# Tile-wise waits on reused places, one transposition on VectorE, and later steps in a decoder trunk

## The chip, the cores and the metric

One core of a Trainium2 chip runs the whole program. The metric is the device time of one execution in microseconds. TensorE is called PE here (PEld its weight loads), VectorE DVE, ScalarE ACT, GpSimd POOL, SyncE SP; transfers are issued from SP.

## What is computed

Two layers on 2048 tokens of width 1024. Layer one: every token is normed and projected to small latents (c_q, c_kv, an index key, index weights, a gate z). An index scores all earlier keys, the best 256 of each query are taken, and eight heads attend to those. Layer two: a gated delta rule with eight heads, chunk by chunk, which needs the inverse of a triangular matrix per chunk. After each layer comes an output projection and a gated embedding of the token. Cut from the reference:

```python
def dsa_mixer(h, ...):
    c_q, c_kv, k_idx, w_idx, z = jnp.split(h @ w_in, ...)
    c_q = rms_norm(c_q, g_cq)
    q_lat = einsum("bshd,hdl->bshl", einsum("bsc,chd->bshd", c_q, w_uq), w_uk)
    q_lat = rms_norm(q_lat, g_q) * (D_C ** -0.5)
    c_kv = rms_norm(c_kv, g_kv)
    score = einsum("bqhs,bqh->bqs", relu(q_idx @ k_idx), w_idx)
    sel = top_k(causal(score), 256)
    o_lat = attention(q_lat, c_kv[sel], rel_bias)
    return (einsum("bshl,hlv->bshv", o_lat, w_uv) * silu(z)) @ w_out
def chunked_gated_delta_rule(q, k, v, g, beta):
    # S_t = a_t S_{t-1} (I - b_t k_t k_t^T) + b_t v_t k_t^T,  o_t = S_t q_t
```

## The kernel before

The program is one stream of steps per engine, written by generators. Each generator yields a number, its place in the stage, and `weave` merges several generators in the order of these numbers; so a constant in a `yield` moves all that stands behind it on every engine. Products of float32 are made as three products of split halves (lines L90, L91, L92 in stage one, L1521 to L1523 in the delta net).

Places in memory come from pools by tag: `T(tag, bufs, ...)` takes the next of `bufs` places of that tag, and waits for whoever used it last. A `scope` opens a pool and gives it back at its end; what is allocated next from the same memory waits for the released pool as a whole.

The stages, by the time of the profile:
- latents (0 to 185 us): `enter` loads a block of 128 tokens (`load_x`), norms it and transposes it (xT, hT); `latents` projects it and norms the results (ncq, nki, nkv; each norm is a sum of squares ss, a root r_t on ACT, a reciprocal r_r on DVE, and a product pb on PE that spreads it). Its last results are written out as ckv_d, and the first scores (il on PE, rl on ACT) are begun with the weights of the gates (w, on ACT line L86).
- scores (185 to 826): `index` (scores), `topk` (a search by halving on POOL, ACT and DVE), and `rest`, which runs `gates_z`, `proj_k`, `proj_v1` and `proj_q`. `proj_q` makes q for a head and 512 tokens (pq, copied to qf and split to q2), and for its norm multiplies it with the Gram matrix of the weights (pgq), then with itself (qg on DVE), then sums (psq on PE). At the end a count of flags is read, and a branch (L671) decides whether a general search is needed.
- attention (830 to 1401): `proj_v` first makes v (pv, v, v_d), then `attend` takes the 16 blocks of queries of each head: logits lg, maximum nm, exponential pr (L1006), transposition pt (L1024) to ph and pl, product po.
- output projection and embedding (to 1822), delta net (to about 3020), output projection again.

In the delta net `within(j)` prepares head-half j (16 of them: 8 heads, two halves of the tokens): kk products (pkk, L1551) give LT, whose blocks go through memory (lt_d, blk) into a 32x32 inversion on DVE, come back as Uc, and are transposed to Tc (L1652). Then blocks of 32 are joined to 64 (px L1664, pd L1673, L1677) and to 128 (px L1684, pd L1689). `across` is the recurrence over eight chunks (pks, y, pu, uu, po, state), `after` norms and transposes the output (vt, pot). Between all of these stand the projections of the next head (pBk, pBq, pBz, pBv).

The lines at the heart of the change are these:

```python
pd = ps("g", 3, f"pd{j}_{p}")
for c in range(NC):
    nc.tensor.matmul(pd[e, c * 32:(c + 1) * 32], X[o, c], Uc[o, c], start=True, stop=True)
nc.scalar.activation(U[e, :, o], pd[e, :NC * 32]..., AF.Copy)
if p == 0:
    for c in range(NC):
        nc.tensor.matmul(pd[o, 256 + c * 32:256 + (c + 1) * 32], Uc[o, c], X[o, c], start=True, stop=True)
    nc.vector.tensor_copy(T64[o, :, 0:32], pd[o, 256:]...)
```

## Time and profile before

| | us |
|---|---|
| median of three runs | 3390.43 (3389.47 to 3390.76) |
| profiled execution | 3399.54 |
| its span in the trace | 3397.4 |
| PE busy | 3288.3 |
| DVE busy | 2113.0 |
| ACT busy | 1858.9 |
| POOL busy | 946.3 |

Busy times are sums over one profiled execution, and its mean granted clock of PE was 0.982 of full speed. PE works in nearly every stretch; a reader looks first at where it waits, and then at the stretches in which the granted clock is about 0.50, the lower of its two levels (1.2 GHz of 2.4 GHz).

### The profile page before, as it was taken

What the parts mean: (1) busy time and instruction counts of PE and PEld (TensorE: products, weight loads), DVE (VectorE), ACT (ScalarE), POOL (GpSimd) and SP (SyncE); (2) the same over time, 40 slices, a digit from 0 to 9 for tenths busy, and PEclk for the clock granted to TensorE, in tenths of its full rate; (3) what the DMA queues carried; (4) which work ended last, traced back from release to release, by engine and by line L of the source; (5) the groups of instructions that cost most, each with busy time, mean ns of one, the idle gap of its engine ahead of it and who ended that gap; (6) DMA issues with size and microseconds to landing.
All of it is one profiled execution on the core that took longest, in us unless ns stands there. A gap on an engine that the chain in (4) does not pass through costs nothing.

```text
span 3397.4 us, 51951 instructions
## 1 busy us (share of the span) xinstructions
PE 3288.3 (97%) x18954; PEld 2769.2 (82%) x18954; DVE 2113.0 (62%) x4502; ACT 1858.9 (55%) x3255; POOL 946.3 (28%) x1620
## 2 busy tenths in 40 slices
PE   8999989998899999999999999999999999899999
PEld 6778877887799999888887888887788888778887
DVE  5358996874788888622225677677677677733222
ACT  5356958674677777533335565555565556433221
POOL 2022545246555445211100221222222232321100
PEclk9999999998999999999999999998999999899999
DMA  7532464543422222422123222222322222333211
GB/s 251 189 101 72 128 205 158 177 162 120 158 77 88 75 82 72 159 81 73 63 65 90 66 57 50 54 60 75 69 57 52 52 60 57 100 126 107 73 40 68
DMA packets 327596, 328.46 MB, mean 97 GB/s; under 512 B 69704, under 2 KB 273064, under 8 KB 323240
## 3 DMA queue, kind: packets, MB, share of 16 engines
q1 hardware_dynamic: 327336, 325.11, 31.7%
q8 instruction: 149, 2.44, 0.3%
q14 instruction: 111, 0.91, 0.1%
HBM read 221.24 MB, written 103.81 MB: 96 GB/s over the span
## 4 chain that ended last, share of the span: by engine, by line
PE 63%; DVE 4%; DMA 4%; ACT 3%; issue 1%; POOL 1%; SPq 0%; DVEq 0%; ACTq 0%; POOLq 0%
PE pgm L91 3%; PE pgm L90 3%; PE pgm L92 3%; PE pt L1024 3%; PE pom L91 2%; PE pom L90 2%; PE pom L92 2%; PE pBv L1521 2%; PE pBv L1523 2%; PE pBv L1522 2%; PE pBk L1521 2%; PE po L1044 2%; PE po L1045 2%; PE pBk L1523 2%; PE lg L92 2%; PE po L1043 2%
## 5 line engine op out<-in xcount | busy, mean ns | idle before, releaser
L78 ACT ACTIVATE ph<-pt 128x512 fp32r<-128x512 f32 (+1 forms) x288 | 162.0, 565 | 107.9 <-PE pt L1024 103.9
L79 DVE TENSOR_TENSOR pl<-pt,ph 128x512 fp32r<-128x512 f32 (+1 forms) x288 | 188.3, 657 | 40.4 <-ACT ph L78 38.5
L1006 ACT ACTIVATE pr<-pr,nm,qscale 128x1024 f32<-128x1024 f32 (+2 forms) x192 | 189.4, 988 | 35.8 <-DVE nm L1003 35.0
L1247 DVE TENSOR_TENSOR gm<-ppm,gm 128x512 f32<-128x512 f32 x64 | 43.4, 690 | 245.1 <-ACT gm L1246 245.1
L423 DVE SCALAR_TENSOR_TENSOR score<-rl,wi,score 128x1024 f32<-128x1024 f32 (+7 forms) x154 | 174.0, 1156 | 32.2 <-ACT rl L415 31.3
L415 ACT ACTIVATE rl<-il 128x1024 f32<-128x1024 f32 (+7 forms) x176 | 142.7, 818 | 72.2 <-PE il L92 64.8
L1024 PE MATMUL pt<-ident,pr 128*128 128x128 f32 x1088 | 168.8, 275 | 9.2 <-ACT pr L1006 4.7
L90 PE MATMUL pom<-wo,ym 128*128 128x512 f32 x432 | 170.4, 394 | 1.9 <-DVE y L1056 1.1
L91 PE MATMUL pgm<-wm,xh 128*128 128x512 f32 x432 | 168.7, 390 | 1.5 <-DVE wm L82 1.5
L91 PE MATMUL pom<-wo,ym 128*128 128x512 f32 x432 | 168.4, 390 | 1.3 <-POOL wo L87 1.3
L90 PE MATMUL pgm<-wm,xh 128*128 128x512 f32 x432 | 168.8, 391 | 0.8 <-ACT gm L1246 0.6
L92 PE MATMUL pgm<-wm,xl 128*128 128x512 f32 x432 | 168.7, 391 | 0.0
L92 PE MATMUL pom<-wo,ym 128*128 128x512 f32 x432 | 168.3, 390 | 0.0
L729 DVE TENSOR_SCALAR_CACHE_REDUCE tkj<-score,t 128x1664 bf16<-128x1664 f32 (+3 forms) x91 | 122.0, 1352 | 71.5 <-POOL t L769 62.1
L87 POOL TENSOR_TENSOR ym<-yr,ym 128x1024 fp32r<-128x1024 f32 x32 | 76.6, 2394 | 314.3 <-ACT ym L86 308.2
L1044 PE MATMUL po<-pl,kv 128*128 128x256 f32 x576 | 162.5, 282 | 1.4 <-DVE pl L79 1.4
L1043 PE MATMUL po<-ph,kv 128*128 128x256 f32 x576 | 162.0, 281 | 0.9 <-ACT ph L78 0.9
L1045 PE MATMUL po<-ph,kv 128*128 128x256 f32 x576 | 161.8, 281 | 0.0
L727 ACT ACTIVATE tkj<-score,t 128x1920 bf16<-128x1920 f32 (+3 forms) x91 | 127.9, 1406 | 28.7 <-POOL t L769 17.4
L1246 ACT ACTIVATE gm<-pgm,rm_r 128x512 f32<-128x512 f32 x64 | 42.9, 685 | 183.8 <-PE pgm L91 117.5
L1024 PEld LDWEIGHTS pt<-ident,pr 128*128 128x128 f32 x1088 | 127.3, 142 | 14.2 <-ACT pr L1006 5.8
L90 PE MATMUL lg<-kv,q 128*128 128x512 f32 (+2 forms) x320 | 138.1, 432 | 0.7 <-DVE mx L997 0.7
(636 smaller groups left out, 10740.7 us busy)
## 6 DMA issues: line engine op xcount, KB each, us to landing
wBr<-in_b_w_in_dram SPq DMA_DIRECT2D x64, 512.0 KB
wr<-in_a_w_in_dram SPq DMA_DIRECT2D x74, 256.0 KB
hT_d<-hT SPq DMA_DIRECT2D x32, 512.0 KB
hz<-hT_d SPq DMA_DIRECT2D x16, 1024.0 KB
yr<-yT_d SPq DMA_DIRECT2D x32, 512.0 KB
x<-in_x_dram SPq DMA_DIRECT2D x16, 512.0 KB
zT_d<-z SPq DMA_DIRECT2D x32, 256.0 KB
k_d<-k SPq DMA_DIRECT2D x16, 512.0 KB
```

The source lines that it names most:

```text
L78: nc.scalar.activation(hi, src, AF.Copy)
L79: nc.vector.tensor_tensor(lo, src, f32(hi), ALU.subtract)
L90: nc.tensor.matmul(dst, ah, bh, start=first, stop=False)
L91: nc.tensor.matmul(dst, ah, bl, start=False, stop=False)
L92: nc.tensor.matmul(dst, al, bh, start=False, stop=last)
L415: nc.scalar.activation(rl[:, :s1 - s0], pl[:, :s1 - s0], AF.Relu)
L423: nc.vector.scalar_tensor_tensor(sc[:, s0:s1], rl[:, :s1 - s0], w, sc[:, s0:s1], ALU.mult, ALU.add)
L1006: nc.scalar.activation(pr[:, s0:s1], pr[:, s0:s1], AF.Exp, bias=nm, scale=sc, accum_out=den[:, i % 2, x:x + 1])
L1024: nc.tensor.transpose(pt[:, x * P:(x + 1) * P], probs[h, i][:, j * P:(j + 1) * P], ident)
L1043: nc.tensor.matmul(d, V[0][:, j], ph[:, c], start=st, stop=False)
L1044: nc.tensor.matmul(d, V[0][:, j], pl[:, c], start=False, stop=False)
L1045: nc.tensor.matmul(d, V[1][:, j], ph[:, c], start=False, stop=sp)
```

## The change

It has several parts. Scopes give their places back tile by tile: what reuses a place waits for the tiles that lay there. In `within` the second group of eight products goes, and DVE transposes the result of the first group from PSUM instead. Norms of x are separate from the loads and stand later in the stream. `proj_q` makes the Gram products two blocks behind in place of one (`LAGQ`); its psc is allocated first, and one Exp activation is written at its end. The v of attention's start take the tags "ph" and "pl" in turn. The gates' first steps and many constants of places move a little.

```diff
         with ExitStack() as st:
-            pools.append(st.enter_context(tc.tile_pool(name=name, bufs=1)))
+            pools.append(st.enter_context(tc.tile_pool(name=name, bufs=1, reuse_waits="tile")))
             if ps:
-                psum = st.enter_context(tc.tile_pool(name=name + "_ps", bufs=1, space=PSUM))
+                psum = st.enter_context(tc.tile_pool(name=name + "_ps", bufs=1, space=PSUM, reuse_waits="tile"))
...
+        return xt
+
+    def norm_x(n, xt):
         ss = sm([P, 1], f"ss{n}")
...
         nc.scalar.activation(junk, xt, AF.Square, accum_out=ss)
         r = rstd(ss, 1.0 / D, 1, f"r{n}")
         nc.vector.scalar_tensor_tensor(xt, xt, r, st1["gain"], ALU.mult, ALU.mult)
-        return xt
...
-        xs = [load_x(sb, b) for b in range(2)]
+        xs, normed = [], 0
+
+        def norms(step):
+            nonlocal normed
+            while normed < len(xs) and 2 * normed - 3 <= step:
+                norm_x(sb * 4 + normed, xs[normed])
+                normed += 1
+
+        for b in range(2):
+            xs.append(load_x(sb, b))
+            norms(-3)
...
+        for s in range(-3, 0):
+            if sb:
+                yield max(0, s / 8 * 0.9492 + 0.0812)
+            norms(s)
...
+                norms(2 * b + i)
...
+                    norms(2 * b + i)
...
-        per = sum(sb * 4 + b + 1 for b in blocks) * 0.1741 + 1.1338
+        per = sum(sb * 4 + b + 1 for b in blocks) * 0.1775 + 1.1338
...
-    LAGQ = 1
+    LAGQ = 2
...
+        psc = T("psc", 1, [P, H, NB], "psc")
         psq = ps("pp", 4, "psq")
...
                 qf = T("raw", 3, [P, SB], f"qf{h}_{sb}", where=pre)
+                q2 = T("w", 4, [P, 2, SB], f"q2{h}_{sb}", F32R)
                 nc.scalar.activation(qf, pq, AF.Copy)
-                q2 = T("w", 4, [P, 2, SB], f"q2{h}_{sb}", F32R)
                 split_sb(qf, q2[:, 0], q2[:, 1])
...
             if n >= LAGQ:
-                yield at + 0.0181
+                yield at + 0.0141
                 m, lq, lf = late.pop(0)
...
-        psc = T("psc", 1, [P, H, NB], "psc")
-
-        nc.vector.tensor_scalar(psc.rearrange("p h b -> p (h b)"), psq[:, :H * NB], 0.0, EPS * 256.0, ALU.max, ALU.add)
+
+        flat = psc.rearrange("p h b -> p (h b)")
+        nc.vector.tensor_scalar(flat, psq[:, :H * NB], 0.0, EPS * 256.0, ALU.max, ALU.add)
         nc.scalar.activation(qinv, psc, AF.Sqrt)
+
+        nc.scalar.activation(small[:, 1:2], eps, AF.Exp)
         nc.vector.reciprocal(qscale, qinv)
...
                     v_block(sb, j, x, ws[j], cs[sb - VB], ps("pt", 3, f"pv{j}_{sb}_{x}"),
-                            T("ph", 2 + AHEAD, [P, 2, 2, P], f"v{j}_{sb}_{x}"))
+                            T("pl" if x else "ph", 2 + AHEAD, [P, 2, 2, P], f"v{j}_{sb}_{x}"))
...
+                    yield -0.1
...
                                 for f in g:
-                                    yield when(w0 + f * w)
+                                    yield max(when(w0 + f * w), 6 if g is gens[0] and w0 == 0 else 0)
...
-    C0, DELTA = 1.269, 8.2959
+    C0, DELTA = 1.4712, 8.2959
...
-        cost = [3.7993 * g + 3 + C0 for _, g in order]
+        cost = [3.5365 * g + 3 + C0 for _, g in order]
...
-            yield -VS + VL * 0.6127
+            yield -VS + VL * 0.6111
...
-    FX = 0.0104
+    FX = 0.0107
...
@@ -1673,9 +1697,7 @@
                     nc.tensor.matmul(pd[e, c * 32:(c + 1) * 32], X[o, c], Uc[o, c], start=True, stop=True)
                 nc.scalar.activation(U[e, :, o], pd[e, :NC * 32].rearrange("p (c n) -> p c n", c=NC), AF.Copy)
                 if p == 0:
-                    for c in range(NC):
-                        nc.tensor.matmul(pd[o, 256 + c * 32:256 + (c + 1) * 32], Uc[o, c], X[o, c], start=True, stop=True)
-                    nc.vector.tensor_copy(T64[o, :, 0:32], pd[o, 256:].rearrange("p (c n) -> p c n", c=NC))
+                    nc.vector.transpose(T64[o, :, 0:32], pd[e, :NC * 32].rearrange("p (c n) -> p c n", c=NC))
...
                 nc.tensor.matmul(px[hi, c * 64:(c + 1) * 64], LT[lo, c, hi], T64[:, c], start=True, stop=True)
             nc.scalar.activation(X[hi].rearrange("p c n -> p (c n)"), px[hi], AF.Copy)
-            yield LV + 0.2043
+            yield LV + 0.1961
             pu = ps("g", 3, f"pd{j}_2")
...
-                t0 = AC + c * AD + (c == NC - 1) * -0.0317
+                t0 = AC + c * AD + {0: -0.0221, 7: -0.0317}.get(c, 0)
...
-                yield t0 + 0.0265 + (0.0243 if c > 1 else 0)
+                yield t0 + 0.0265 + {2: 0.0243, 3: 0.0243, 4: 0.0243, 5: 0.0243, 6: 0.0243, 7: 0.0243}.get(c, 0)
...
-            yield from by4(f"pot{j}", transposes(o), o_sink, at + 0.0469)
+            yield from by4(f"pot{j}", transposes(o), o_sink, at + 0.0469, -0.004)
...
-                at = 0.5842 + x * 0.25 if part == 0 else x / n
+                at = 0.6523 + x * 0.25 if part == 0 else x / n
...
-    VS, VL, V0, V1 = (40.0, 39.3825, 38.628, 20)
+    VS, VL, V0, V1 = (40.0, 38.6473, 38.628, 20)
```

The order of the instructions moves with it at these places.

PE, the joining of the inverse in head-half 2 (pd and X, Uc: the blocks of 32; pBv: the projection of v of the next head), before and after:

```order
L1521 MATMUL pBv3_1_22939<-hB0_0_20410,wB15_22788 128x512
L1673 MATMUL pd2_0_22947<-Uc2_22836,X2_0_22891 32x32 x8
L1673 MATMUL pd2_1_22966<-Uc2_22836,X2_0_22891 32x32 x8
L1522 MATMUL pBv3_1_22939<-hB0_0_20410,wB15_22788 128x512
L1523 MATMUL pBv3_1_22939<-hB0_0_20410,wB15_22788 128x512
L1677 MATMUL pd2_0_22947<-X2_0_22891,Uc2_22836 32x32 x8
L1521 MATMUL pBv3_1_22939<-hB0_1_20411,wB15_22788 128x512
```

```order
L1545 MATMUL pBv3_1_22924<-hB0_0_20411,wB15_22773 128x512
L1697 MATMUL pd2_0_22932<-Uc2_22821,X2_0_22876 32x32 x8
L1697 MATMUL pd2_1_22943<-Uc2_22821,X2_0_22876 32x32 x8
L1546 MATMUL pBv3_1_22924<-hB0_0_20411,wB15_22773 128x512
L1547 MATMUL pBv3_1_22924<-hB0_0_20411,wB15_22773 128x512
L1545 MATMUL pBv3_1_22924<-hB0_1_20412,wB15_22773 128x512
```

The group L1677 is gone, and the products of pBv follow one another; the next small products (px) stand after eight of them.

ACT, the end of the latents and the beginning of the scores (nkv3o: the last latents; w41, w43, w45: weights of the gates; rl3: the first scores), before and after:

```order
L81 ACTIVATE nkv3o1_1595<-nkv3cr4_1541,a_g_kv_94 128x512
L86 ACTIVATE wiq3_2_1805<-wiq_raw3_2_1803 128x256
L86 ACTIVATE w41_1649<-wr40_1647 128x512
L86 ACTIVATE w43_1654<-wr42_1652 128x512
L86 ACTIVATE w45_1659<-wr44_1657 128x512
L415 ACTIVATE rl3_0_0_0_1674<-il3_0_0_0_1667 128x1024
L415 ACTIVATE rl3_0_0_1024_1690<-il3_0_0_1024_1683 128x640
L78 ACTIVATE qi_1599<-qi3_1_1699 128x512
```

```order
L81 ACTIVATE nkv3o1_1595<-nkv3cr4_1541,a_g_kv_94 128x512
L86 ACTIVATE wiq3_2_1805<-wiq_raw3_2_1803 128x256
L78 ACTIVATE qi_1599<-qi3_1_1693 128x512
L435 ACTIVATE rl3_0_0_0_1641<-il3_0_0_0_1634 128x1024
L86 ACTIVATE w41_1659<-wr40_1657 128x512
L86 ACTIVATE w43_1664<-wr42_1662 128x512
L86 ACTIVATE w45_1669<-wr44_1667 128x512
L435 ACTIVATE rl3_0_0_1024_1684<-il3_0_0_1024_1677 128x640
```

The first rl and the copy of qi now stand ahead of the three weight splits.

DVE, the kk products of head-half 3 (LT: their scaled copies; state, vt: the recurrence of head-half 2; rs: the norm of an earlier output; wB17: a weight split), before and after:

```order
L1594 SCALAR_TENSOR_TENSOR LT3_23025<-pkk3_0_23086,ncj3_23062,dT3_23065 128x128 x4
L1600 RECIPROCAL rs3_23027<-rs3_23027 128x8
L1594 SCALAR_TENSOR_TENSOR LT3_23025<-pkk3_1_23102,ncj3_23062,dT3_23065 128x128 x4
L1762 SCALAR_TENSOR_TENSOR state_20791<-state_20791,cd2_22386,po2_0_23128 128x128
L1764 COPY vt2_22596<-po2_0_23128 128x128
L1319 TENSOR_TENSOR wB17_23138<-wBr17_23081,wB17_23138 128x1024
```

```order
L1618 SCALAR_TENSOR_TENSOR LT3_23002<-pkk3_0_23063,ncj3_23039,dT3_23042 128x128 x4
L1784 SCALAR_TENSOR_TENSOR state_20792<-state_20792,cd2_22371,po2_0_23079 128x128
L1786 COPY vt2_22581<-po2_0_23079 128x128
L1624 RECIPROCAL rs3_23004<-rs3_23004 128x8
L1343 TENSOR_TENSOR wB17_23116<-wBr17_23058,wB17_23116 128x1024
L1618 SCALAR_TENSOR_TENSOR LT3_23002<-pkk3_1_23085,ncj3_23039,dT3_23042 128x128 x4
```

The second half of LT has moved behind state, vt, rs and the weight split. On SP the four transfers lt_d<-LT stand one weight transfer later. Of the added Exp activation ACT's order shows this: it and a table load of its own stand second among ACT's instructions, ahead of the first xsq, and behind that xsq comes one more table load, for the square root of the first norm (L161).

## Rows read from the trace of the kernel before

**Rows 1.** The page's busy times by engine, with share of the span and instruction count.

```profile
PE 3288.3 (97%) x18954; PEld 2769.2 (82%) x18954; DVE 2113.0 (62%) x4502; ACT 1858.9 (55%) x3255; POOL 946.3 (28%) x1620
```

**Rows 2.** PE's waits: us in total, times, longest.

```profile
PE il L90 <- ACT rl L415: 7.2, 3, 5.9
...
PE pt L1024 <- ACT pr L1006: 4.7, 1, 4.7
...
PE ncq2pb L281 <- DVE ncq2r_r L163: 3.7, 1, 3.7
...
PE pgq L91 <- POOL q L87: 3.4, 4, 1.1
...
PE psq L477 <- DVE qg L509: 2.9, 5, 0.9
...
PE px L1664 <- DVE Tc L1652: 2.9, 3, 2.2
```

**Rows 3.** Timeline of PE at 2202 to 2204 us: start, us, then the instruction.

```profile
2202.51 0.40 PE L1523 MATMUL pBv<-hB,wB 128*128 128x512 f32 x1
2202.84 0.69 PE L1677 MATMUL pd<-X,Uc 32*32 32x32 f32 x16
2203.45 0.50 PE L1521 MATMUL pBv<-hB,wB 128*128 128x512 f32 x1
2203.79 0.40 PE L1522 MATMUL pBv<-hB,wB 128*128 128x512 f32 x1
2204.02 0.40 PE L1523 MATMUL pBv<-hB,wB 128*128 128x512 f32 x1
```

**Rows 4.** Lines L1678 and L1652 on DVE: duration in ns (min/median/max).

```profile
L1678 DVE COPY T<-pd x16: 417/418/420, 1931.5 to 2987.3; 32x256 f32<-32x256 f32 x16
...
L1652 DVE STREAM_TRANSPOSE Tc<-Uc x16: 435/446/448, 1923.5 to 2981.6; 128x256 f32<-128x256 f32 x16
```

**Rows 5.** Timeline around ncq2's norm.

```profile
115.83 1.02 PE L276 MATMUL ncq2ss<-ones,ncq2sq 128*128 128x1 f32 x8
...
122.54 0.24 ACT L161 ACTIVATE ncq2r_t<-ncq2ss,small 128x4 f32<-128x4 f32 x1
```

**Rows 6.** Timeline of ACT at 191 us; in brackets the idle time before.

```profile
190.98 1.67 ACT L86 ACTIVATE w<-wr 128x512 fp32r<-128x512 f32 x3 [5.05 <-DMA ckv_d<-nkv3o]
192.56 1.60 ACT L415 ACTIVATE rl<-il 128x1024 f32<-128x1024 f32 x2
```

**Rows 7.** Windows: length, busy us of PE, PEld, DVE, ACT, POOL; granted clock; DMA.

```profile
192.60:199.40 6.80, 5.63 (x12) 3.99 (x13) 3.32 (x3) 1.55 (x3) 3.77 (x3) 0.50 0.98 410
2066.50:2069.90 3.40, 3.40 (x13) 2.36 (x14) 0.42 (x1) 0.00 (x0) 0.00 (x0) 0.50 0.45 75
2984.80:2998.20 13.40, 13.40 (x73) 10.12 (x71) 1.64 (x2) 3.80 (x7) 0.00 (x0) 0.50 0.01 2
```

**Rows 8.** Timeline of ACT behind the branch and before the first exponential.

```profile
830.34 1.67 ACT L86 ACTIVATE wv<-wvr 128x512 fp32r<-128x512 f32 x3 [4.12 <-DVEq L671]
...
851.52 0.60 ACT L561 ACTIVATE v<-pv 128x512 f32<-128x512 f32 x1 [1.46 <-DMA v_d<-v]
...
853.06 1.28 ACT L1006 ACT_TABLE_LOAD   x1
854.35 0.49 ACT L1006 ACTIVATE pr<-pr,nm,qscale 128x128 f32<-128x128 f32 x1
```

**Rows 9.** Timeline: the flags of the last search on DVE.

```profile
823.71 0.15 DVE L806 TENSOR_TENSOR flags<-got,want 128x2 f32<-128x2 f32 x1
```

**Rows 10.** Timeline of LT's way in head-half 3.

```profile
2012.20 1.13 DVE L1594 SCALAR_TENSOR_TENSOR LT<-pkk,ncj,dT 128x128 f32<-128x128 f32 x4
...
2018.86 0.32 SPq L1613 DMA_DIRECT2D blk<-lt_d  x1
...
2022.60 2.11 POOL L1622 COPY blk<-blk 32x1024 f32<-32x1024 f32 x2
...
2027.94 0.17 DVE L1627 COPY low<-blk 128x16 f32<-128x16 f32 x1
```

More of the change, by code (lines that the diff above doesn't have):

```diff
@@ L346, in gates_z @@
             hT += [t[:, 0], t[:, 1]]
-        ws, order = {}, [(c, kh, x) for c in range(0, H, 2) for kh in range(2) for x in range(2)]
+        order = [(c, kh, x) for c in range(0, H, 2) for kh in range(2) for x in range(2)]
+        ws = {}
         def ahead(n):
@@ L365, in gates_z @@
                     for x in range(2):
-                        mm3_step(pz[x], w[x][:, 0, k], w[x][:, 1, k], hT[kh * 4 + k][:, 0], hT[kh * 4 + k][:, 1],
+                        h = hT[kh * 4 + k]
+                        mm3_step(pz[x], w[x][:, 0, k], w[x][:, 1, k], h[:, 0], h[:, 1],
                                  kh == 0 and k == 0, kh == 1 and k == 3)
@@ L407, in index @@
                     s1 = min(n, s0 + 1024)
-                    at += (s1 - s0) / P * 0.1741
+                    at += (s1 - s0) / P * 0.1775
                     pl = ps("il", 2, f"il{sb}_{b}_{h}_{s0}", 1024)
@@ L1306, in load_weights @@
     def load_weights(n):
-        half, h, i = n // 32, n // 4 % H, n % 4
+        h, i = n // 4 % H, n % 4
         c = (8 * P, 0, 3088, 16 * P)[i] + h * P
@@ L1699, in beside @@
             nc.scalar.activation(aq.rearrange("p c n -> p (c n)"), qT, AF.Square)
+            sq = sm([P, NC], f"sq{j}", tag="sq", bufs=3)
             yield 0.22
@@ L1704, in beside @@
                 nc.tensor.matmul(pq2[:, c:c + 1], aq[:, c], ones[:, 0:1], start=True, stop=True)
-            sq = sm([P, NC], f"sq{j}", tag="sq", bufs=3)
             nc.vector.tensor_scalar(sq, pq2[:, 0:NC], EPS, EPS * P, ALU.add, ALU.mult)
@@ L1843, in tile_trunk @@
     VB = 3
-    RO = "zkq"
+    RO = 'zkq'
     WQ = 90.0
     WK = 42.0
-    VS, VL, V0, V1 = (40.0, 39.3825, 38.628, 20)
+    VS, VL, V0, V1 = (40.0, 38.6473, 38.628, 20)
     PLAN = ({3: (0, 120), 2: (120, 256), 1: (294, 400), 0: (418, 470)}, {3: (122, 300), 2: (302, 415), 1: (417, 483), 0: (482, 534)}, 518)
```

## The prediction

> **What bounds the kernel now.** I read the table of busy time first, then TensorE's waits, the granted clock by stretch, and the timeline around each place that the change touches. TensorE (PE) is busy for 3288.3 of 3397.4 us [rows 1], no other engine above 62%. So the end moves by three things only: work taken off PE, PE's idle time (3397.4 - 3288.3 = 109 us), and stretches in which PE works at the lower clock level. The waits [rows 2] name where much of the idle time lies: 5.9 us once at the end of the latents (il), 4.7 us at attention's first transposition (pt), 3.7 us in the latents (ncq2pb), 3.4 and 2.9 us in the projection of q (pgq, psq). The clock [rows 7] shows what a wait costs beyond itself: after PE had stood for 5.9 us it worked for 6.8 us at 0.50 of 2.4 GHz, so 3.4 us were lost again. Small products come before such stretches too: right behind the 32x32 products of a head PE has 3.4 us at 0.50 in which it is busy throughout.
>
> The sum is made against the profiled execution, 3399.5 us; the median of the runs is 3390.4, so 9.1 us go off the result.
>
> **Part 1, the transposition (VectorE, DVE, for eight products).** In each of 16 head-halves the group L1677 goes. The product before it starts at 2202.51, the next one at 2203.45: 0.94 us [rows 3]; the same products with nothing between them stand 0.23 us apart (2203.79 to 2204.02). That is 0.71 us of PE time, and the product after that one starts 0.34 us later instead of 0.23, another 0.11: 0.82 us. Fourteen head-halves show the same 0.94; the two others ran at the low clock and lose about 1.2 us each. 14 x 0.82 + 2 x 1.2 = 13.9 us; by the 0.71 alone, and 1 us for the two, 11.9 us. I take **12.5**. On DVE a copy of 418 ns goes and a transposition comes; the existing one, on four times as many partitions, takes 446 ns [rows 4]. It can start earlier, since it no longer waits for L1677, and its reader (px, L1684) stands eight products behind its source, 8 x 0.23 = 1.8 us. The source is PSUM, where the trace has no transposition; at twice 446 ns it would still be done before px.
>
> Does the clock gain as well? Four head-halves have 3.4 us at 0.50 behind L1677 (one of them stands in [rows 7]), and two have 13.4 us (one of them there), half of each lost: 4 x 1.7 + 2 x 6.7 = 20 us at most, nothing at least. The other 32x32 products stay, so I take a tenth, **2**.
>
> **Part 2, finer waits at the scope boundaries.** At the end of the latents ScalarE (ACT) stood 5.05 us for the DMAs ckv_d<-nkv3o before its weight splits, and the rl stood behind these [rows 6]; PE's il waited 5.9 us for that rl [rows 2]. Now the first rl waits only for the place it reuses, written out long before, and stands ahead of the splits; the second one still waits for the ckv_d DMAs, so until about 191. In between PE has six products of qi and one group of six of il, 12 x 0.23 = 2.8 us. Of 5.9 us some 1.6 should be left: 4.3 us, and half of the 3.4 us that the clock took, 1.7: **6** (if the second rl keeps everything but half the products: 2; if all of the clock's loss goes too: 9).
> Behind the branch ACT's wv stood 4.12 us [rows 8]; most of that is the branch, a fifth, 0.9 us, the wait of every engine for every other, which goes; SP's transfers start sooner with it. In attention's first blocks ACT's v waited 1.46 us for a DMA that empties its place, then came the table load, 1.28 us, then the first exponential [rows 8] that PE's pt waited for, 4.7 us. With v on two tags the 1.46 goes, and an earlier k_d brings another 1.5 or so. On the other side the pl of attention use the same places, and now wait for v's DMAs. 0.9 + 3 of the 4.7: **4** (from -2, if pl's new waits cost two of 1.46 and little else comes, to 9 with the clock). At the three later boundaries no single wait of PE reaches the 2.9 us that is the least in rows 2: an estimate of **1** (0 to 2).
>
> **Part 3, later norms of x.** PE's ncq2pb waited 3.7 us [rows 2] for a reciprocal whose input ncq2ss was there at 115.83 + 1.02 = 116.85, while ACT's next step on it ran at 122.54 [rows 5], behind the norm of another block of x on ACT and DVE. In the new order it stands ahead of that norm. 3.7 us, and half of the clock's loss behind it (3.4 us at 0.50, so 0.8): **4.5** (1, if PE only meets the next norm; 5.4 with all of the clock's).
>
> **Part 4, q's Gram products two blocks behind.** The waits pgq and psq are 3.4 + 2.9 = 6.3 us [rows 2]. Lag two gives POOL and DVE a block of PE's work more, nine products at 0.23 us, so 2.1 us, against single waits of at most 1.1: they should go. But the stage ends on the top-k search as well: its flags come at 823.71 [rows 9], and its steps run on POOL, ACT and DVE whatever PE does. About half is kept: **3.5** (0 to 8, with the clock).
>
> **Part 5, the small ones.** Gates of z later at their start: six more products, 6 x 0.23 = 1.4 us, stand in front of one wait of PE: **1** (0 to 1.4). The Exp activation that is written at the end of q's projection stands, in the built order, among ACT's first instructions, and brings one load more for the square root behind it; the load before attention stays. So it doesn't do what it says. A load takes 1.28 us [rows 8], here on the chain of the first block of x, part of which the second block's wait for its DMA takes up: **-0.6** (-1.3 to 0).
> The Trainium skill (ScalarE: Activation LUTs, What ACT_TABLE_LOAD costs) puts a switch at 2.66 us, with a drain after the load; the next ACTIVATE starts 1.29 us after the load does [rows 8], so the trace shows no such drain. By the page the term would be -2 at the middle and the sum 1.4 us less.
> In the head-halves of the delta net DVE now does the state, vt, rs and a weight split before the second half of LT, and lt_d<-LT stands behind a weight DMA on SP. LT's second half stood at 2012.20 [rows 10]; from the length of the steps put ahead of it I work out 2.2 us of delay, half of which reaches blk, since blk stood in SP's queue until 2018.86 anyway. DVE's next step on blk is at 2027.94 in its own queue, while the copies of blk end at 2022.60 + 2.11 = 2024.71 [rows 10]: 3.2 us of cover against 1.1, so nothing is left over. rs is 0.7 us later for the output's transpositions (pot): **-1** (-7, if 14 head-halves lose half a us; +5, if the earlier state shortens the recurrence's waits).
>
> **The sum.** 12.5 + 2 + 6 + 4 + 1 + 4.5 + 3.5 + 1 - 0.6 - 1 = 32.9 us. 3399.5 - 32.9 = 3366.6, less 9.1: **3357 us**.
>
> **Rivals.**
> *The clock keeps its losses.* The terms 2, 1.7 and 0.8 rest on fewer low stretches. If shorter gaps only move them, the sum is 28.4, and the time 3362. For it: of sixteen head-halves in the same order of products, most show no low stretch there, four 3.4 us and two 13.4.
> The Trainium skill (TensorE: Matmul & The Clock Gate, What's actually happening) has the clock's monitor run free of the kernel, so that the point of a change varies; by that the clock's terms are chance and the time is this rival's, and the trace agrees in so far as like head-halves differ.
> *The waits are replaced.* Each start of a stage has several late things in a row: behind rl the ckv_d DMAs, behind ncq2pb the next norm, behind psq the search, behind v the table load. If the next one is about as late, only part 1 is sure, with 3 us of parts 2 and 3: 12.5 + 3 - 0.6 - 1 = 13.9 us, 3376. For it: the second rl does wait for the same DMAs. Against it: at ncq2pb the data were there 5.7 us before they were used.
> *Lag two lacks places.* The tag raw has three, and a head's weights take one of them, so qf of two blocks in each of 8 heads waits until qg of two blocks before is done: three products and a step of DVE, about 1.6 us. If PE doesn't cover it, 16 x 1.6 = 26 us, and the time is 3383: no change. Against it: PE needs that q two blocks later.
> *The inverse comes late: slower than before.* From LT to Tc it is one chain through two DMAs, and px waited for Tc in 3 of 16 head-halves already [rows 2], so there is little room at its end. If LT's 2.2 us went through, PE would wait some 1.7 us in 14 head-halves, 24 us, and the last one shows what can follow such a wait: 2.2 us of it [rows 2], then 13.4 us at 0.50 [rows 7], 6.7 us lost. With that behind half of them, 24 + 7 x 6.7 = 71 us: 3428. It decides from 3.2 us of lateness at blk; my estimate is 1.1.
>
> **How the numbers follow.** Forecast 3357: 0.45. Clock kept, 3362: 0.20. Waits replaced, 3376: 0.19. Lag two lacks places, 3383: 0.10. Inverse late, 3428: 0.06. With part 1 at 13.9 and the other parts at their good ends the time would be under 3340, and I don't expect all of them together; with parts 2 to 5 near their bad ends it is 3382. Range 3336 to 3382. A measurement of this kernel can tell 0.2%, 6.8 us: faster is below 3383.6. The first three cases give faster 0.84, the fourth the same 0.10, the last slower 0.06.
>
> **What would show it.** In the changed profile: no 32x32 product between the pBv products and these 0.23 us apart, DVE's transposition under 0.9 us; il's wait near 188 under 2 us; ncq2pb without a wait; pgq and psq gone from the list, a wait for the flags in their place; pt's wait under 2 us; px's waits for Tc no longer than before. The prediction is wrong if px or pot wait in every head-half, qf waits for DVE in the projection of q, or the low stretches of the clock stay as long without a wait ahead of them.

## The result, and the profile of the kernel after

| | before | after |
|---|---|---|
| median, us | 3390.6 (3389.47 to 3391.25, 4 runs) | 3354.97 (3350.8 to 3356.83, 4 runs) |
| profiled execution, us | 3399.54 | 3356.33 |
| its span and mean granted clock | 3397.4, 0.982 | 3354.6, 0.988 |

The ratio of after to before is 0.9894, with an interval of 0.9876 to 0.9911: 35.6 us less, where 33 were forecast (3357 us). The busy times of after, from the page's first part, answer [rows 1]:

```profile
PE 3259.4 (97%) x18698; PEld 2750.0 (82%) x18698; DVE 2112.6 (63%) x4502; ACT 1857.0 (55%) x3258; POOL 943.8 (28%) x1620
```

The 256 matmuls of L1677 are gone (the trace counts two for each product), and PE is busy for 28.9 us less. Its idle time falls from 109.1 us to 3354.6 - 3259.4 = 95.2. PE's waits in after (total, times, longest, in us), beside [rows 2]:

```profile
PE xT L219 <- DVE r_r L163: 9.0, 1, 9.0
...
PE pt L1048 <- ACT pr L1030: 3.3, 2, 2.8
...
PE il L90 <- ACT rl L435: 2.9, 3, 1.6
PE px L1688 <- DVE Tc L1676: 2.5, 3, 1.4
...
PE pq L90 <- DVE qi L79: 1.9, 2, 1.2
...
PE pq L90 <- DVE qg L530: 1.8, 4, 0.9
...
PE psq L498 <- DVE qg L530: 1.5, 2, 1.3
```

The longest il goes from 5.9 to 1.6, pt from 4.7 to 2.8, and px waits no longer than before. ncq2pb is not in the list any more, nor is pgq's wait for q. New are the waits of pq, and the first xT, which came after 7.6 us, now comes after 9.0.

How each stage fared, in the two profiled executions. A stage reaches from the first product of one name to the first of the next; "low" is the time in which PE was busy at a granted clock of about 0.50. All three columns are worked out from every matmul and every clock record of the traces; over the whole span low time fell from 103.7 us to 69.9.

| stage | length, us | PE idle, us | low, us |
|---|---|---|---|
| start to il (latents) | 185.1, now 179.6 | 15.8, 13.3 | 3.4, 0 |
| il to pk (scores) | 392.1, 384.8 | 22.1, 16.6 | 18.6, 16.6 |
| pk to pq | 125.6, 124.5 | 5.2, 4.1 | 0, 0 |
| pq to pf (projection of q) | 122.8, 123.0 | 6.5, 6.4 | 4.5, 3.2 |
| pf to pt (branch, first v) | 29.5, 27.0 | 11.0, 8.6 | 6.4, 6.1 |
| pt to pom (attention) | 547.2, 548.0 | 11.5, 9.7 | 8.9, 13.9 |
| pom to pBk | 421.4, 420.7 | 5.5, 4.6 | 0, 0 |
| pBk to poe (delta net) | 1118.7, 1098.8 | 19.0, 21.7 | 46.9, 19.9 |
| poe to PE's last product | 449.9, 443.1 | 7.4, 5.1 | 15.1, 10.2 |

Two things stand out. The projection of q gained nothing. And in the delta net low time fell by 27 us, worth half of that at most, 13.5, where I had put 2.

**Work and clock apart.** Each execution comes with its time and its mean granted clock. Executions of one and the same kernel differ: among 36 of before, beside the experiments, one took 3391.55 us at 0.985, the slowest 3411.21 at 0.979. Over all 104 executions of the table below, each held against the mean of its kernel in the same group of runs, a fitted line gives 2.4 us less for each 0.001 of clock (standard error 0.15), and explains three quarters of the scatter. So the experiments read better at equal clock: the last column is the mean time, less 2.4 us for each 0.001 by which the kernel's mean clock lies below after's. The uncertainty of such a mean is about 1 us.

| kernel | executions | mean time | mean clock | at after's clock |
|---|---|---|---|---|
| before | 36 | 3396.7 | 0.9821 | 3381.4 |
| after | 4 | 3354.4 | 0.9885 | 3354.4 |
| e1 before, transposition alone | 5 | 3379.3 | 0.9836 | 3367.6 |
| e2 after, the eight products again | 7 | 3380.2 | 0.9841 | 3369.7 |
| e10 before, the eight products twice | 6 | 3407.6 | 0.9815 | 3390.8 |
| e12 before, finer waits alone | 12 | 3389.3 | 0.9827 | 3375.3 |
| e4 after, without finer waits | 6 | 3368.0 | 0.9858 | 3361.6 |
| e7 after, v on one tag | 4 | 3356.0 | 0.9872 | 3353.0 |
| e5 after, norms early | 4 | 3358.8 | 0.9872 | 3355.8 |
| e3 after, lag one | 4 | 3355.6 | 0.9865 | 3350.8 |
| e9 after, gates early | 4 | 3357.2 | 0.9882 | 3356.6 |
| e8 after, delta order undone | 4 | 3354.1 | 0.9885 | 3354.1 |
| e6 after, no Exp | 4 | 3358.3 | 0.9872 | 3355.3 |
| e13 after, Exp hidden | 4 | 3354.2 | 0.9882 | 3353.6 |

Against before's mean after is 42.3 us shorter: 27.0 at equal clock, 15.3 by the clock. The traces give nearly the same split without the line: taking half a us as lost for each us of low time, what is left of the span falls by 25.9 us from before to after and by 13.8 from before to e1, and rises by 15.9 from after to e2 and by 8.7 from before to e10. Only for the finer waits is it less, 4.7 us (e12) and 3.8 (e4). These are single executions.

Ratios below are against before as it was timed beside the experiment; its median was 3390.6 beside after and 3394.7 to 3397.4 beside the experiments (three chips), so kernels that were timed apart are compared by this table.

### The profile page after: what moved, and what is told of

Its sections match the earlier page's. It is cut to its first block, busy times and chain, and to the rows that moved or that the text cites. A ratio compares the mean times of both kernels' runs of the same rounds, so it can differ in the third digit from the quotient of the medians.

```text
span 3354.6 us, 51369 instructions
## 1 busy us (share of the span) xinstructions
PE 3259.4 (97%) x18698; PEld 2750.0 (82%) x18698; DVE 2112.6 (63%) x4502; ACT 1857.0 (55%) x3258; POOL 943.8 (28%) x1620
## 4 chain that ended last, share of the span: by engine, by line
PE 47%; DVE 4%; DMA 3%; ACT 2%; POOL 1%; issue 1%; SPq 0%; DVEq 0%; ACTq 0%; POOLq 0%
PE pgm L91 3%; PE pgm L90 3%; PE pgm L92 3%; PE pom L90 2%; PE pom L91 2%; PE pom L92 2%; PE pBv L1545 2%; PE pBv L1547 2%; PE pBv L1546 2%; PE pBq L1545 1%; PE pBq L1547 1%; PE pBq L1546 1%; PE pBk L1545 1%; PE pBk L1547 1%; PE pBk L1546 1%; PE pBz L1545 1%
## 5 line engine op out<-in xcount | busy, mean ns | idle before, releaser
L1030 ACT ACTIVATE pr<-pr,nm,qscale 128x1024 f32<-128x1024 f32 (+2 forms) x192 | 189.4, 988 | 33.8 <-DVE nm L1027 31.9
```

The source lines that it names most:

```text
L1030: nc.scalar.activation(pr[:, s0:s1], pr[:, s0:s1], AF.Exp, bias=nm, scale=sc, accum_out=den[:, i % 2, x:x + 1])
```

## The experiments

**Part 1: the eight products.** The transposition alone, put into before:

```diff
-    for c in range(NC):
-        nc.tensor.matmul(pd[o, 256 + c * 32:256 + (c + 1) * 32], Uc[o, c], X[o, c], start=True, stop=True)
-    nc.vector.tensor_copy(T64[o, :, 0:32], pd[o, 256:]...)
+    nc.vector.transpose(T64[o, :, 0:32], pd[e, :NC * 32]...)
```

> The kernel before with part 1 alone (DVE transposes the first group, the eight products L1677 go). Theory A (PE time that goes, 0.71 to 0.87 us in each of 16 head-halves, and a little clock): 12.5 + 2 us less, about 3376, ratio 0.9957. Rival B (the small products also bring the low stretches of the clock in the delta net, 47 us of them in that stage before, so most of those go too): 12 + 13 us less, about 3365, ratio 0.9926. Rival C (DVE or px late, the gain is lost): ratio 0.999 or more. The profile tells A from B: low stretches behind the 32x32 products as before, or gone.

Ratio 0.9955 (0.9942 to 0.9969), 15.3 us less: at equal clock 13.0 (3380.6 for before beside it, less 3367.6), the rest clock. By the time theory A holds. The low time in the delta net, by which the profile was to tell A from B, is 23.8 us in e1, about half of before's 46.9, so this one profile has something of B in it. e2 is the reverse edit, in after:

> The changed kernel with the eight products L1677 back and the copy in place of the transposition. Theory A: 12.5 to 14.5 us slower than the changed kernel, about 3368. Rival B (clock goes with the products): 22 to 27 us slower, about 3380. Rival C (all comes from elsewhere): within 3 us of the changed kernel, 3355.

Ratio 0.9955 (0.9939 to 0.997); 25.8 us slower than after by the mean times, 15.3 at equal clock. The work is near A's; the whole is B's, for the clock falls from 0.9885 to 0.9841, and the low time in the delta net is 43.5 us where after has 19.9. To price the products by themselves, e10 issues them twice (same places, same values):

```diff
-    for c in range(NC):
+    for c in [*range(NC), *range(NC)]:
         nc.tensor.matmul(pd[o, 256 + c * 32:256 + (c + 1) * 32], Uc[o, c], X[o, c], start=True, stop=True)
```

> Before with the eight 32x32 products that turn the inverse's blocks issued twice into the same places, in all 16 chunks; the values are the same, so that only the price of the group changes. Before's profile has the group at 0.69 us on PE (0.78 us of path in the sum). Theory A (the work is what it seems, and the clock follows such small products): 16 x 0.69 to 0.78 = 11 to 12.5 us slower, and the busy time at the low clock in the delta stage above before's 46.9 us, up to 20 us more of it, which would cost up to 10 us: 11 to 22 us slower, ratio 1.0032 to 1.0065. Rival B (the group is hidden beside the wait for the next step of the inverse, and its removal gained by shortening the chain of semaphores alone): 0 to 4 us, ratio 1.000 to 1.0012. Rival C for the clock: the work costs 11 to 12.5 us and the low-clock time in the stage does not rise (below 50 us).

Ratio 1.0034 (1.0021 to 1.0047): 8.7 us at equal clock (against before's 3382.1 beside it), less than the 11 to 12.5 that A and C gave. PE's timeline at the same place in e10 (start, us, instruction), to be held against [rows 3]:

```profile
2201.97 0.40 PE L1523 MATMUL pBv<-hB,wB 128*128 128x512 f32 x1
2202.30 1.19 PE L1677 MATMUL pd<-X,Uc 32*32 32x32 f32 x32
2203.42 0.50 PE L1521 MATMUL pBv<-hB,wB 128*128 128x512 f32 x1
```

From L1523 to L1521 it is 1.45 us instead of 0.94: the second group costs 0.51, and 16 x 0.51 = 8.2 us. So the price is PE's, no chain of semaphores behind it. The first group costs 0.71, the changeover to small products and back included. The low time in the delta net was 36.4 us, below before's 46.9, and the mean clock hardly moved (0.9815 against 0.9819). Of the clock's theories C came true: issuing the group twice did not bring more time at the low level.

Where these stretches begin is another matter, and all fourteen traces show it. In the delta net's head-halves 35 low stretches begin at a group of 32x32 products (pd), within 1 us of the start of one. In after, for example:

```profile
2870.59 1.16 PE L1697 MATMUL pd<-Uc,X 32*32 32x32 f32 x32
2871.68 0.79 PE L1546 MATMUL pBv<-hB,wB 128*128 128x512 f32 x1
```

```profile
2871.50:2874.90 3.40, 3.40 (x14) 2.59 (x11) 1.68 (x3) 2.52 (x5) 0.00 (x0) 0.50 0.00 0
```

The second row has length, busy time of PE, PEld, DVE, ACT and POOL, granted clock (0.50) and DMA. Of the 35, 16 lie in the four kernels that issue L1677's group and 19 in the ten that do not; PE's low time in them is 31.6 and 15.1 us on average (17.1 to 41.0, and 10.2 to 27.3). Nine of the 16 begin at L1677's group itself; before's four of these (3.4 us each) come when PE has been busy without a gap for 127 us or more, so no wait brings them. Those at the first group, which stays, are about as frequent with it (7 in four) as without (19 in ten).

**Part 2: finer waits.** Alone, in before (no instruction moves), and the reverse in after:

```diff
-            pools.append(st.enter_context(tc.tile_pool(name=name, bufs=1)))
+            pools.append(st.enter_context(tc.tile_pool(name=name, bufs=1, reuse_waits="tile")))
```

(and the same for PSUM's pools)

> Before with finer waits on reused places alone; no instruction is moved on any engine. Theory A (the second part of the sum): 2 to 9 us at the boundary at 187 us, -2 to 9 at the branch and the attention's start, 0 to 2 at three later ones; after without them was 8 us slower than after, of which its profile puts 5 us at boundaries. So 5 to 9 us faster than before, ratio 0.9973 to 0.9985, with PE's longest wait of il on ACT's rl below 4 us instead of 7.2 and fewer than 2 us of low clock behind it. Rival B (the waits take effect only together with the moved norms and gates, which free the places earlier): under 3 us, ratio 0.9991 or above, the wait of il on rl still 6 us or more.

> The changed kernel with pools that wait as a whole at the scope boundaries; the order of instructions is that of the changed kernel. Theory A (the waits are the gain at the boundary near 187 us and behind the branch): 6 to 9 us slower than the changed kernel, about 3363, il waiting 4 to 6 us again for rl. Rival B (the new order of ACT alone is the gain, rl ahead of the weight splits): under 2 us slower, il waits as in the changed kernel.

e12: ratio 0.9976 (0.9961 to 0.9991), 8 us less, of which 6.8 at equal clock (from 3382.1): A. e4: ratio 0.9918 (0.9904 to 0.9932), 7.2 us slower than after at equal clock, and 6.4 more by the clock. PE's waits in e12 around 187 us, then ACT there:

```profile
PE pz L90 <- DMA hz<-hT_d: 4.0, 1, 4.0
PE il L90 <- ACT rl L415: 0.8, 1, 0.8
PE il L90 <- ACT qi L78: 0.7, 1, 0.7
```

```profile
185.09 1.66 ACT L86 ACTIVATE w<-wr 128x512 fp32r<-128x512 f32 x3
186.65 1.01 ACT L415 ACTIVATE rl<-il 128x1024 f32<-128x1024 f32 x1
190.24 0.70 ACT L415 ACTIVATE rl<-il 128x640 f32<-128x640 f32 x1 [2.58 <-DMA ckv_d<-nkv3o]
```

The splits w, which had waited 5.05 us for ckv_d [rows 6], wait no more, and the first rl follows at once; only the second rl meets the DMA. But PE gains little by it. Behind the il it now stands 4.0 us, until 193.14, for the load of hz, which the gates' first products (pz) read; in before PE came to pz only at 196.28 and hardly waited (0.2 us). With the old waits in after (e4), the first rl stands for it, in the new order too, but for less:

```profile
185.26 1.02 ACT L435 ACTIVATE rl<-il 128x1024 f32<-128x1024 f32 x1 [1.43 <-DMA ckv_d<-nkv3o]
```

il's longest wait is 5.9 us in before, 3.1 with the new order but the old waits (e4; theory A had 4 to 6), 0.8 with the waits alone (e12), 1.6 with both. What counts is all of PE's idle time at this place (176 to 201 us): 7.0 us in before, 5.7 in e12, 3.4 in e4, 1.8 in after, and 5.9 in e9 (below), which has the finer waits and the gates at their old place. So the gates' later start brings most of the gain here (4.1 us), and the finer waits 1.3 to 1.5. The rest of what the finer waits are worth lies elsewhere, and e12 and e4 do not agree on where: in e4 PE is idle for 1.8 us more than in after from pk to pq and 2.4 more in attention, while e12 has 0.6 more than before in the first and 1.3 less in the second.

The low stretch, of which less than 2 us had been expected, is also there in e12 (length, busy time of PE, PEld, DVE, ACT, POOL, granted clock, DMA):

```profile
191.50:198.40 6.90, 5.26 (x13) 4.12 (x13) 1.33 (x2) 0.00 (x0) 2.46 (x2) 0.51 1.01 424
```

It begins while PE stands for hz. In the fourteen traces the low stretch at this place goes with PE's longest wait there: where that was 4.0 us or more (before, e1, e9, e10, e12) 6.8 us or more follow at the lower level, behind e4's 3.1 us it is 3.4, and behind 1.6 us it is 3.4 in two kernels of eight and nothing in six.

e7 puts all v of attention's start back on the tag "ph":

> The changed kernel with all v of attention's start on the tag ph again. Theory A (v waits for the DMA that empties its place, ahead of the exponentials): ACT's v waits 1 to 1.5 us for v_d, pt's wait 2 us longer, 2 us slower (3357). Rival B (the new waits of pl for v's DMAs cost what the two tags give): within 1 us, pt's wait for pr longer and its waits for pl shorter.

Ratio 0.9875 (0.9858 to 0.9892): in the time nothing to be told. At its place it is as said; ACT in e7 shortly before the first exponential (at 840.14):

```profile
837.74 1.09 ACT L584 ACTIVATE v<-pv 128x512 f32<-128x512 f32 x2 [1.58 <-DMA v_d<-v]
```

v waits again for a DMA, pt for 5.3 us instead of 2.8, and pv to pt takes 2.1 us more (24.07 against 21.94).

**Parts 3 to 5.** e5 puts x's norms back into `load_x`, and ahead of the projections:

```diff
-        return xt
-    def norm_x(n, xt):
...
-            xs.append(load_x(sb, b))
-            norms(-3)
+        xs = [load_x(sb, b) for b in range(2)]
```

> The changed kernel with each norm of x right behind its load. Theory A (ncq2pb meets the norm again): from the start to the first il 3.5 to 6 us longer, 183 to 186 us, ncq2pb waiting 3 to 4 us, time 3360. Rival B (the finer waits or the moved gates made the gain): under 1.5 us, no wait at ncq2pb.

Ratio 0.9886 (0.987 to 0.9903); 4.4 us more than after by the mean times, 1.4 of them at equal clock, which its uncertainty doesn't set apart from nothing. The latents take 6.6 us longer (186.22 against 179.59): 2.8 us of idle time, ncq2pb's 3.7 among it, and 12.3 us of low time where after has none. The scores behind them give 4.2 us back, by shorter waits (1.5 us) and less low time. In after the root follows its sum at once, where [rows 5] had 5.7 us between them:

```profile
116.85 0.26 ACT L161 ACTIVATE ncq2r_t<-ncq2ss,small 128x4 f32<-128x4 f32 x1 [2.64 <-PE ncq2ss L294]
```

e3 sets `LAGQ = 1` with its old place:

> The changed kernel with q's Gram products one block behind again (LAGQ 1 and its old place). Theory A (lag two gives nothing: the stage from the first pq to pf is 122.8 us before and 123.0 after, since new waits of pq for qg stand where pgq waited for q, and the search runs its own pace): within 2 us of the changed kernel, stage 122 to 124 us. Rival B (lag two gave 3 to 4 us, and something else in the change took them back): 3 to 4 us slower, stage 126 to 127 us, with waits of pgq for q.

Ratio 0.9877 (0.9861 to 0.9894), 3355.6 us against after's 3354.4. PE's waits of the projection of q in e3:

```profile
PE pgq L91 <- POOL q L87: 3.0, 4, 1.1
PE psq L498 <- DVE qg L530: 2.9, 5, 0.9
```

They are back, 5.9 us, and the stage takes 123.5 us instead of 123.0. With lag two PE waits about as long for other things: its idle time is 6.4 us in after, 6.1 in e3. In after's list pq waits 1.8 us for qg and 1.9 for qi, psq still 1.5. Not the search's flags: in after they come at 810.74, ahead of the end of the last psq. ACT's waits in this stage have a new one too; in before's there is none of qf for qg:

```profile
ACT qf L517 <- DVE qg L530: 4.7, 6, 1.3
```

e9 takes the gates' first steps back:

```diff
-                    yield -0.1
...
-                                    yield max(when(w0 + f * w), 6 if g is gens[0] and w0 == 0 else 0)
+                                    yield when(w0 + f * w)
```

> The changed kernel with the first steps of the gates at their old place, so that on ACT the three weight splits stand ahead of the first rl again; the waits stay tile by tile. Theory A (the finer waits alone are the gain at 187 us, since the splits then wait for nothing late): within 2 us of the changed kernel, 3355 to 3357. Rival B (the order counts, since the splits wait for the ckv_d DMAs even tile by tile): 4 to 6 us slower, about 3360, il waiting about 5 us.

Ratio 0.9886 (0.987 to 0.9902), 2.2 us more at equal clock, hardly beyond its uncertainty. The order counts, but not by the wait that rival B named: il's longest is 0.9 us, and pz waits twice for hz (9.0 us in all, after 4.7), once as in e12, behind that il.

e8 puts the delta net's constants back (`FX`, `LV`, `t0`, pot's lead, the projection's start):

> After with the hand-set places of the delta net put back: the figure that spreads the work, the place of the gate's last vector product, the first transfer's place, the lead of the out transpositions and the start of the output projection are before's. Everything else is after's. After's profile has the delta stage (first pBk to first poe) at 1098.82 us and the rest to the end at 443.13, before's 1118.74 and 449.94. Theory A (the new places are worth about nothing, -1 of the sum with ends of -7 and +5): this kernel is within 3 us of after, ratio to before 0.9885 to 0.991, the two stages together 1540 to 1546 us in its profile once the busy time at the low clock is set aside. Rival B (the places carry what the work of the eight products does not explain, 5 to 8 us): ratio 0.9910 to 0.9930, the two stages together 1547 to 1551, and PE's waits ahead of the output projection's first products longer than after's 1.8 us each.

Ratio 0.9878 (0.9863 to 0.9893), 3354.1 us: nothing, as A said. The delta net took 1096.5 us and the rest 445.7, in all 0.3 more than after.

e6 leaves out the Exp. e13 puts it where it could have served, behind the first v past the branch, and has it read that v so that it can't be issued sooner:

```diff
-        nc.scalar.activation(small[:, 1:2], eps, AF.Exp)
...
         nc.scalar.activation(t, pv.rearrange("p (b h v) -> p h b v", b=2, h=2), AF.Copy)
+        if (sb, j, x) == (VB, 0, 0):
+            nc.scalar.activation(small[:, 1:2], t[:, 0, 0, 0:1], AF.Exp, scale=1e-6)
```

> The changed kernel without the added Exp activation. Theory A (it stands at the start and costs a table load on the first norm): the first xT starts at 7.6 us instead of 8.96, the first table load before attention stays at 1.28 us, time 0.5 to 1.5 us less, about 3354. Rival B (the load at the start lies in a wait for x): first xT at 8.9 as in the changed kernel, same time. Rival C (it does spare a load before attention): pt later by 1.3 us, time 1 us more.

> After with the Exp whose only purpose is to bring ACT's table early taken from its place behind the square root and put behind the copy of the first v tile past the branch, reading that tile, so that it cannot be issued earlier. In the order of ACT's instructions the two extra table loads at the start are gone, and the load stands between the first and the second copy of v, where ACT was idle for 1.75 us in after's profile. Expected if the step is right: the first xT at about 7.6 us instead of 8.96, no table load ahead of the first pr, the stretch from the first pv to the first pt 0.5 to 1.3 us shorter than after's 21.94; 1.3 to 2.6 us less than after in all, ratio to before 0.9882 to 0.9890 if after is at 0.9894, below what the timing of one kernel against another can settle. Rival: the start is given back by the next wait (the loads of x or of the weights), the time is after's, and only the first xT moves.

e6: ratio 0.9878 (0.9861 to 0.9894), first xT at 7.70 us; at equal clock it takes 0.9 us more than after, where theory A had 0.5 to 1.5 less. e13: 0.9875 (0.9859 to 0.9891). ACT at the start of after, then past the branch in e13:

```profile
2.30 1.28 ACT L539 ACT_TABLE_LOAD   x1
3.60 0.20 ACT L539 ACTIVATE small<-small 128x1 f32<-128x1 f32 x1
4.54 1.06 ACT L185 ACTIVATE xsq<-x 128x1024 bf16<-128x1024 f32 x1 [0.74 <-DMA x<-in_x_dram]
...
5.71 1.28 ACT L161 ACT_TABLE_LOAD   x1
```

```profile
820.99 0.60 ACT L583 ACTIVATE v<-pv 128x512 f32<-128x512 f32 x1 [3.36 <-PE pv L92]
821.61 1.28 ACT L585 ACT_TABLE_LOAD   x1
822.90 0.20 ACT L585 ACTIVATE small<-v 128x1 f32<-128x1 f32 x1
823.01 0.62 ACT L86 ACTIVATE wv<-wvr 128x512 fp32r<-128x512 f32 x1
```

The second load at the start stands on the chain to xT and goes with e6 and e13; in e13 the load moves into time in which ACT was idle, pv to pt falls from 21.94 to 19.56 us, and the first xT comes at 7.71. That is 3.6 us at the two places; the mean time is 3354.2 us against 3354.4, at equal clock 0.8 less. The places agree with the forecast, a faster kernel is not shown.

## Why the prediction was right, step by step

By kind, the sum of 32.9 us was 28.4 of work and waits, and 4.5 of clock (2, 1.7 and 0.8). Against before's mean it is 27.0 and 15.3. The two profiled executions say the same: low time fell by 33.8 us, worth 16.9; PE's busy time fell by 28.9, which leaves 12.0 for the products (12.5 in the sum); and PE's idle time fell by 13.9, where the other terms of work and waits make 15.9. So the work was right as a whole, the clock was too small by 11 us, and the time came out because the three runs of before, to whose median I came down by the 9.1 us, lay 6 us below the mean of the 36 later executions. That part is luck, and why those three were faster is not shown.

- **Part 1, work 12.5: right.** 13.0 (e1) and 15.3 (e2) at equal clock, 8.2 for a group right behind another (e10). The transposition from PSUM, bounded at twice 446 ns, takes 440 ns, and nobody waits for it:

```profile
L1700 DVE STREAM_TRANSPOSE T<-pd x16: 439/440/440, 1912.9 to 2946.4; 32x256 f32<-32x256 f32 x16
```

- **Part 1, clock 2 of up to 20: the term that was mis-sized.** I took a tenth since the other small products stay. The low time in the delta net fell by 27 us in the profiled executions, and in all the clock is worth 15. The stretches that begin at L1677's group itself are what goes with it: nine in four traces, 37.5 us of PE's low time, so 9.4 in an execution and 4.7 us of loss. The reason for the tenth holds for the rest, which begin at the group that stays; my two long ones of 13.4 us are of that kind and not "behind L1677". Beyond that the gain is shown only in part, and not by addition: against before beside them the transposition alone is worth 2.5 us of clock (e1), the finer waits alone 2 (e12); but taking the first out of after costs 10.5 (e2), taking out the second 6.4 (e4). e10 speaks against the small products as the cause by their number. Low time in the delta net was 23.0 us in e12 too, which has all the products, and 36.9 in e4, which has none of L1677; so a single profile does not settle it, and 4.7 is an average over few traces. Why the clock's losses go when several edits meet stays open.
- **Part 2, the boundary at 187 us, 6: right at its place, but mostly by another edit.** "Some 1.6 should be left" is what il waits. The finer waits alone take 1.3 us off PE's idle time there (e12), since hz comes late next; the gates' later start, which I priced at 1 under part 5, takes 4.1 (e9). The low stretch behind it went from 6.8 us to 3.4, as the sum had it, and it does go with the wait. But PE was busy for 5.63 of the 6.80 us [rows 7], so 2.8 us was lost there and not 3.4. **Branch and attention's start, 4:** 2.5 us by the stages (pf to pt). The wv's wait fell from 4.12 to 3.64 us, by half of the 0.9 I gave it; the load before the exponential stayed, and pt's wait did not come under 2 us, as it should have (2.8). **Later boundaries, 1: perhaps too small.** PE's idle time fell by 1.1 us from pk to pq, 1.8 in attention and 0.9 from pom to pBk, and in e4 the first two are back (1.8 and 2.4 us more than after). With the waits alone (e12) the first does not fall and the others fall by 1.3 and 0.5, so how much is theirs is not shown.
- **Part 3, 4.5: right at its place, half as much in the whole.** The wait went, and e5 gives 4.4 us with an uncertainty of about 2; but 1.4 of it is left at equal clock where I had 3.7, since the next stage waits less when this one waits more.
- **Part 4, 3.5: wrong.** It is 0 by the times (e3: 1.2 us more than after; at equal clock 3.6 less). pgq's wait went, psq's 2.9 us became 1.5, and new ones of pq for qg and qi took their place. The rival of the missing places shows in small: qf waits on ACT for qg, the sign that I had named, but six times and for 4.7 us in place of 26; and PE's own wait for qg is for a place of PSUM that qg frees (the tag pp), which I had left out. The reason that I gave for keeping half, that the search ends last, is not what the trace of after shows.
- **Part 5: right within its bounds.** The Exp doesn't do what it says and costs 1.3 us at the first xT (e6); in the whole time this can't be told. The gates, 1: 2.2 in the whole, with an uncertainty of 1.6, and 4.1 at their place. The delta net's new order, -1: nothing (e8). Its idle time did grow by 2.6 us, but in e1, in the old order, by 4.0; that PE reaches its next waits sooner without the products would fit, but is not shown.

Of the rivals, "the clock keeps its losses" missed by the sign of its doubt: the losses fell by more than I had allowed. "The waits are replaced" holds for part 4, in part for part 3, and for the finer waits by themselves at 187 us. The late inverse did not come: px's longest wait is 1.4 us, where it was 2.2. Taking 9.1 us off because the profiled execution stood so far above the median rested on three runs that lay close together; at 0.982 its clock was before's ordinary one.

## What to carry to other kernels

Read the granted clock of every execution beside its time, and compare kernels at equal clock as well: an edit of 8 us could be placed so where one kernel's spread was 20. A wait that goes is worth only what the next one in the same row leaves, so look for that one in the trace before the term is written down; in the projection of q it took all, and with the finer waits alone a load that came next took 4.0 of the 5.1 us that il no longer waited. And an instruction that is to bring a table early must read something that is made late, or the order puts it first.

## What was not expected of the hardware

The mean granted clock of one and the same kernel ran from 0.978 to 0.985 over 36 executions, and with it went much of its spread of 3390.3 to 3411.2 us. What the edits gave in clock was not a sum (about 0.001 for either of two alone, 0.0064 for all), and 128 more small products left it nearly as it was. Low stretches in the delta net's head-halves began, 35 of them in fourteen traces, within 1 us of the start of a 32x32 product; before four of them in the kernel before PE had been busy for 127 us or more without a gap.
